# Grouping the last two groups' stores into one transfer of 64 KB pieces, and splitting gamma into two transfers, in an RMSNorm-GELU kernel

## The chip, the cores and the metric

One core of one Trainium2 chip. The metric is the device time of one execution in microseconds (us), as a median over runs; the span in a profile is the same execution seen by the hardware profiler and is about 1.8 us shorter.

## The reference

```python
# x: (8, 1024, 2048) float32, gamma: (2048,), eps = 1e-5
rms = np.sqrt(np.mean(x ** 2, axis=-1, keepdims=True) + eps)
out = gamma * x / rms
return 0.5 * out * (1 + np.tanh(np.sqrt(2 / np.pi) * (out + 0.044715 * out ** 3)))
```

8192 rows of 2048 floats are read once and written once: 67.1 MB in and 67.1 MB out.

## The kernel before

The rows are cut into 16 groups of 512 rows: 128 partitions with 4 rows each, 4 MB. Six slots of 4 MB hold groups in SBUF, as three tiles of two slots. SyncE issues the loads, ScalarE gamma and the stores. Per group, ScalarE and VectorE share the squares, a few small operations give the inverse root, VectorE multiplies by gamma (held in PSUM, spread there by TensorE), ScalarE does the GELU in place, and the slot is stored. The next load into a slot waits for that store.

Two neighbouring groups can be laid out as a pair: each partition then holds 8 consecutive rows, so one transfer of 8 MB moves 64 KB in one piece per partition instead of 32 KB. Before the change that is done for the load of groups 2 and 3 and for the store of groups 12 and 13.

```python
LOAD_PAIR = 1
STORE_PAIR = 6
GW = 128
...
    def part(a, g):
        if g // 2 in (LOAD_PAIR, STORE_PAIR):
            return pair_part(a, g // 2)[:, g % 2 * R : g % 2 * R + R, :]
        return a[g * R * P : (g + 1) * R * P].rearrange("(p r) d -> p r d", p=P)
...
    spare = sbuf.tile([P, D // GW, GW + 16], FP32, name="spare")   # scratch of VectorE's squares
    gamma_row = spare[0:1]                                         # gamma lands there first
...
    def store(g):
        if g:
            if g // 2 != STORE_PAIR:
                nc.scalar.dma_start(out=part(o2, g), in_=slot[g % SLOTS])
            elif g % 2:
                nc.scalar.dma_start(
                    out=pair_part(o2, g // 2), in_=pair[g // 2 % (SLOTS // 2)])
            return
        ...  # group 0: two transfers
...
        for g in range(G + 1):
            if g < G:
                squares(g, 0, R - on_vector(g))
                squares_on_vector(g, R - on_vector(g), on_vector(g))
                ...  # inverse_rms(g), scale(g)
            if g:
                gelu(g - 1)
                store(g - 1)
                if g - 1 + SLOTS < G:
                    load(g - 1 + SLOTS)
```

## Time and profile before

| | before |
|---|---|
| time, median of the first 3 runs | 316.97 us (316.78 to 317.06) |
| span of the profiled run | 315.1 us |
| busiest compute engines | ScalarE 66%, VectorE 63% |
| both DMA queues together | 99.0% of the 16 engines' span |
| bytes moved | 134.24 MB, 426 GB/s over the span |

The row to look at first in such a page is the one of the DMA, because no compute engine comes near its span. In the wait lists, the columns are the engine and line that waited, what it waited for, the sum in us, how often and the longest. Stretches of the DMA ("windows") count a packet wholly where it starts. A packet here is one piece of 32 or 64 KB and takes 1.2 or 2.4 us. Holes were therefore read from the packet records themselves. The lines of the kernel before are in the prediction below.

### The profile page before, as it was taken

How to read it: one execution, taken by the hardware profiler on the slowest of the kernel's cores; microseconds unless marked ns; L12 is line 12 of the kernel's file. 1: busy time of each engine (PE TensorE's matmuls, PEld its weight loads, DVE VectorE, ACT ScalarE, POOL GpSimd, SP SyncE). 2: the span in 40 equal slices, each digit the busy share in tenths (PEclk: the TensorE clock that was granted, in tenths of full speed). 3: DMA queues.
4: the chain of work that ended last, by engine and by line, in shares of the span. 5: the costliest groups of instructions: out<-in, count | busy, mean ns of one | idle time of the engine just before them, and what ended most of it. 6: DMA issues, size and time to landing. Idle time of an engine off the chain costs nothing.

```text
span 315.1 us, 457 instructions
## 1 busy us (share of the span) xinstructions
PE 7.2 (2%) x8; PEld 2.5 (1%) x8; DVE 198.5 (63%) x129; ACT 206.9 (66%) x150; POOL 16.4 (5%) x21
## 2 busy tenths in 40 slices
PE   0900000000000000000000000000000000000000
PEld 0300000000000000000000000000000000000000
DVE  0089887988989884639684393668727638781000
ACT  1327869999999749397590965929369295797000
POOL 0010101011010101010010100101001010010000
DMA  8999989999999999999999999999999999999896
GB/s 334 404 462 408 526 339 396 458 402 462 403 463 403 459 408 458 412 453 424 441 424 441 424 441 424 441 428 437 437 428 437 428 437 428 474 399 474 387 445 291
DMA packets 4498, 134.24 MB, mean 426 GB/s; under 512 B 512, under 2 KB 656, under 8 KB 656
## 3 DMA queue, kind: packets, MB, share of 16 engines
q1 hardware_dynamic: 2160, 67.11, 49.7%
q10 hardware_dynamic: 2336, 67.12, 49.3%
q14 instruction: 2, 0.02, 0.0%
HBM read 67.12 MB, written 67.11 MB: 426 GB/s over the span
## 4 chain that ended last, share of the span: by engine, by line
another core or an unknown queue 36%; DMA 36%; ACT 18%; issue 1%; SPq 1%; ACTq 0%
DMA pair<-in_x_dram 21%; DMA out_dram<-pair 15%; ACT pair L133 12%; ACT junk L87 6%; SPq L83 1%; ACTq L143 0%
## 5 line engine op out<-in xcount | busy, mean ns | idle before, releaser
L124 DVE TENSOR_TENSOR pair<-pair,gamma_ps 128x8192 f32<-128x8192 f32 (+1 forms) x19 | 139.2, 7334 | 0.0
L87 ACT ACTIVATE junk<-pair 128x2048 f32<-128x2048 f32 x42 | 79.0, 1881 | 78.7 <-DMA pair<-in_x_dram 76.2
L133 ACT ACTIVATE pair<-pair,rstd 128x2048 f32<-128x2048 f32 x64 | 122.6, 1987 | 2.3 <-DVE pair L124 1.9
L97 DVE SCALAR_TENSOR_TENSOR spare<-pair 128x2048 f32<-128x2048 f32 x22 | 50.4, 2291 | 39.3 <-DMA pair<-in_x_dram 24.6
L110 POOL TENSOR_TENSOR y<-ms,power 128x4 f32<-128x4 f32 x16 | 16.1, 1007 | 260.8 <-DVE ms L105 260.8
L105 DVE TENSOR_SCALAR ms<-ssq 128x4 f32<-128x4 f32 x16 | 2.7, 170 | 26.2 <-ACT junk L87 25.4
L113 DVE TENSOR_TENSOR z<-ms,y 128x4 f32<-128x4 f32 x16 | 2.6, 163 | 19.0 <-POOL y L110 19.0
L87 ACT ACTIVATION_READ_ACCUMULATOR junk<-pair 128x1 f32 x42 | 7.8, 186 | 0.0
L171 PE MATMUL gamma_ps<-spare,ones 1*128 1x512 f32 x8 | 7.2, 1072 | 8.3 <-DMA spare<-in_gamma_dram 8.3
L117 DVE SCALAR_TENSOR_TENSOR rstd<-z,y 128x4 f32<-128x4 f32 x16 | 2.6, 162 | 0.6
L114 DVE SCALAR_TENSOR_TENSOR z<-z,y 128x4 f32<-128x4 f32 x16 | 2.6, 162 | 0.6
L171 PEld LDWEIGHTS gamma_ps<-spare,ones 1*128 1x128 f32 x8 | 2.5, 326 | 11.4 <-issue 11.4
L169 ACT ACT_TABLE_LOAD x1 | 1.3, 1283 | 1.4 <-PEq L211 1.4
L97 DVE DVE_READ_ACCUMULATOR spare<-pair 128x1 f32 x22 | 1.8, 83 | 0.0
L167 DVE MEMSET warm<- 1x1 f32 x1 | 0.1, 59 | 0.8 <-PEq L211 0.8
L169 ACT ACTIVATE warm<-warm 1x1 f32<-1x1 f32 x1 | 0.2, 202 | 0.0
L168 DVE MEMSET ones<- 1x128 f32 x1 | 0.2, 165 | 0.0
L166 POOL MEMSET power<- 128x4 f32 x1 | 0.1, 101 | 0.3 <-POOLq L211 0.3
L211 POOL MEMSET const-float32-0.0<- 128x1 f32 x1 | 0.1, 98 | 0.2 <-issue 0.2
L211 POOL MEMSET const-bfloat16-1.0<- 128x1 bf16 x1 | 0.1, 102 | 0.0
L211 POOL MEMSET const-uint8-127<- 128x1 uint8 x1 | 0.1, 102 | 0.0
L211 POOL MEMSET const-float32-1.0<- 128x1 f32 x1 | 0.1, 98 | 0.0
## 6 DMA issues: line engine op xcount, KB each, us to landing
pair<-in_x_dram SPq DMA_DIRECT2D x14, 4096.0 KB, 25.5
out_dram<-pair ACTq DMA_DIRECT2D x13, 4096.0 KB, 52.4
out_dram<-pair ACTq DMA_DIRECT2D x1, 4032.0 KB, 31.3
out_dram<-pair ACTq DMA_DIRECT2D x1, 64.0 KB, 17.6
spare<-in_gamma_dram ACTq DMA_DIRECT2D x1, 8.0 KB, 7.4
pair<-in_x_dram SPq DMA_DIRECT2D x1, 40.5
out_dram<-pair ACTq DMA_DIRECT2D x1, 30.9
```

The lines of the kernel that those rows point to most:

```text
L83: nc.sync.dma_start(out=slot[g % SLOTS], in_=part(x2, g))
L87: nc.scalar.activation(out=junk, in_=slot[g % SLOTS][:, q, :], func=ACT.Square, accum_out=ssq[:, g, q : q + 1],)
L97: nc.vector.scalar_tensor_tensor(out=spare[:, :, 0:GW], in0=row, scalar=1.0, in1=row, op0=ALU.bypass, op1=ALU.mult, accum_out=ssq[:, g, q ...
L105: v.tensor_scalar(out=ms, in0=ssq[:, g, :], scalar1=1.0 / D, scalar2=eps_f, op0=ALU.mult, op1=ALU.add,)
L110: nc.gpsimd.tensor_tensor(out=y_, in0=m_, in1=power, op=ALU.pow)
L113: v.tensor_tensor(out=z_, in0=m_, in1=y_, op=ALU.mult)
L114: v.scalar_tensor_tensor(out=z_, in0=z_, scalar=-0.5, in1=y_, op0=ALU.mult, op1=ALU.mult)
L117: v.scalar_tensor_tensor(out=rstd[:, g, :], in0=z_, scalar=1.5, in1=y_, op0=ALU.add, op1=ALU.mult,)
L124: nc.vector.tensor_tensor(out=rows, in0=rows, in1=gamma_ps.unsqueeze(1).to_broadcast([P, n, D]), op=ALU.mult,)
L133: nc.scalar.activation(out=slot[g % SLOTS][:, r, :], in_=slot[g % SLOTS][:, r, :], func=ACT.Gelu_apprx_tanh, scale=rstd[:, g, r : r + 1],)
L169: nc.scalar.activation(out=warm, in_=warm, func=ACT.Gelu_apprx_tanh)
L171: nc.tensor.matmul(out=gamma_ps[:, k : k + 512], lhsT=ones, rhs=gamma_row[:, k // GW : (k + 512) // GW, 0:GW], start=True, stop=True,)
```

## The change

Groups 14 and 15 are stored as a pair, as groups 12 and 13 already are, and gamma is loaded in two halves, with the scratch tile cut to fit. Its intent: fewer and longer pieces at the end, where nothing but stores runs, while the number of transfers stays at 32. The diff is shortened.

```diff
-STORE_PAIR = 6
-GW = 128
+STORE_PAIRS = (6, 7)
+GW = 64
+GAMMA = [(0, 1024), (1024, 2048)]
@@ part
-        if g // 2 in (LOAD_PAIR, STORE_PAIR):
+        if g // 2 in (LOAD_PAIR, *STORE_PAIRS):
@@
-    spare = sbuf.tile([P, D // GW, GW + 16], FP32, name="spare")
+    spare = sbuf.tile([P, D // GW, GW + 8], FP32, name="spare")
@@ store
-            if g // 2 != STORE_PAIR:
+            if g // 2 not in STORE_PAIRS:
@@
-        nc.scalar.dma_start(
-            out=gamma_row[:, :, 0:GW],
-            in_=gamma.rearrange("(o a b) -> o a b", o=1, b=GW),
-        )
+        for a, b in GAMMA:
+            nc.scalar.dma_start(
+                out=gamma_row[:, a // GW : b // GW, 0:GW],
+                in_=gamma[a:b].rearrange("(o a b) -> o a b", o=1, b=GW),
+            )
```

## The prediction

> **What bounds the kernel now.** I read first the shares of the engines, the DMA row over time and the queue table (the page of the kernel before):
>
> ```profile
> PE 7.2 (2%) x8; PEld 2.5 (1%) x8; DVE 198.5 (63%) x129; ACT 206.9 (66%) x150; POOL 16.4 (5%) x21
> DMA  8999989999999999999999999999999999999896
> DMA packets 4498, 134.24 MB, mean 426 GB/s; under 512 B 512, under 2 KB 656, under 8 KB 656
> q1 hardware_dynamic: 2160, 67.11, 49.7%
> q10 hardware_dynamic: 2336, 67.12, 49.3%
> ```
>
> No compute engine is above 66%. The two queues, q1 (loads, issued by SyncE) and q10 (gamma and stores, issued by ScalarE), together fill 49.7 + 49.3 = 99.0% of the 16 DMA engines' span of 315.1 us, so about 3 us of the span (1%) are without transfers. The bytes are fixed: 67.1 MB in, 67.1 MB out.
>
> Second, the waits, of ScalarE and of SyncE's own queue:
>
> ```profile
> ACT junk L87 <- DMA pair<-in_x_dram: 76.2, 12, 10.1
> ACT pair L133 <- DVE pair L124: 1.9, 1, 1.9
> SPq L83 <- DMA out_dram<-pair: 236.9, 11, 47.3
> ```
>
> ScalarE's 78.7 us of idleness before its squares is waiting for loads; the loads wait for stores to free their slots. All of it is the DMA.
>
> Third, the tail, which the change touches: the timeline of ScalarE and its queue, and the DMA share in stretches (columns: stretch, its length, busy time of PE, PEld, DVE, ACT, POOL, clock, DMA share, GB/s).
>
> ```profile
> 264.01 0.34 ACTq L145 DMA_DIRECT2D out_dram<-pair  x1
> ...
> 281.29 0.34 ACTq L143 DMA_DIRECT2D out_dram<-pair  x1
> 281.67 7.68 ACT L133 ACTIVATE pair<-pair,rstd 128x2048 f32<-128x2048 f32 x4 [0.42 <-ACT pair L133]
> 289.38 0.34 ACTq L143 DMA_DIRECT2D out_dram<-pair  x1
> ```
> ```profile
> 264.00:281.00 17.00, 0.00 (x0) 0.00 (x0) 13.01 (x12) 11.32 (x8) 1.01 (x1) 1.00 1.01 436
> 281.00:289.00 8.00, 0.00 (x0) 0.00 (x0) 3.90 (x2) 7.58 (x5) 0.00 (x0) 1.00 1.04 451
> 293.60:313.00 19.40, 0.00 (x0) 0.00 (x0) 0.00 (x0) 0.00 (x0) 0.00 (x0) 1.00 1.00 432
> ```
>
> The store of groups 12 and 13 (8 MB) goes out at 264.0, group 14's at 281.3, group 15's at 289.4, and nothing computes after that. Yet the DMA is full from 264 to 313: the last stores wait behind a backlog. The page's row of issues gives 30.9 us from issue to landing for the 8 MB store, that is 294.9. So the two 4 MB stores, issued at 281.3 and 289.4, cannot begin before about 294.
>
> I then took the packet records (start, length and size of every packet) and chained packets into 16 engines by matching ends to starts. On every engine a packet starts 4 ns before the last one ends; I found no gap above 0.13 us. The engines begin between 1.74 and 2.91 us and end between 312.98 and 313.93 us; they finish the 8 MB store between 293.6 and 294.6 us. The span is thus: 1.74 us to the first byte, some 312 us of packets without a hole, and 1.16 us from the last packet to the end.
>
> [...] a packet of 32,768 bytes takes 1,213 ns, less the 4 ns of overlap, so 27.1 GB/s for one engine and 433.7 for 16. [...] 65,536 bytes take 2,418 ns, two packets of half the size 2,426, so about 8 ns a packet, or 4 ns net of the overlap. [...] gamma's 16 packets of 512 B start at 5.9 to 6.6 us, its 16 completion writes at 7.2 to 7.8, one 32 KB load packet between the two. [...] The page of the kernel before has 2,291 ns for N = 2048 where the output is cut into 16 pieces[...].
>
> **The change part by part.**
>
> *The two last stores become one of 8 MB.* Removed: one issue of 0.34 us on ScalarE at 281.3, and 256 packets of 32 KB. Added: 128 packets of 64 KB. On each engine 16 x (1,213 - 4) = 19,344 ns become 8 x (2,418 - 4) = 19,312 ns: 32 ns less. One completion write per engine goes: 9 - 4 = 5 ns less. Group 14's data now wait for group 15's gelu, some 8 us longer, but this costs only if an engine runs dry first. The last gelu no longer waits for the issue at 281.3: its rows are ready on VectorE at 280.5, 282.7 and 284.9 us, so the four activations of about 1.92 us run from 281.3 to about 289.0. The store is issued at 289.0, done at 289.3. A first packet on an idle queue followed its issue within 1.0 us at the start (0.74 to 1.74), which gives 290.0. The first engine runs out of the 8 MB store at 293.6: 3.6 us to spare. So no hole; -0.04 us at the end.
>
> *The loads of groups 14 and 15* take rows with the stride of the pair: still 128 pieces of 32 KB each, as groups 12 and 13 already have, whose packets took the same 1,213 ns. No cost.
>
> *Gamma in two transfers.* 16 packets of 512 B (27 ns each, one per engine) become 32 of 256 B (about 18 ns, an estimate from 9 ns for a 4-byte packet and 27 for 512 B). Per engine 2 x (18 - 4) - (27 - 4) + 5 for one more completion write = +10 ns. With one load packet between each, as above, the second half's completion comes two load packets after the first's: 2 x 1.2 = 2.4 us, so near 10.2 us, 10.6 as seen by TensorE. The first half feeds the first four of eight matmul records, which at 7.16/8 = 0.9 us keep TensorE busy from 8.3 to 11.8 us. The second half is there by then, and gamma's broadcast still ends at 15.4.
>
> *32 transfers in all.* One store fewer and one gamma transfer more keep the count. The compiled program hands eight completion semaphores out in turn, and a transfer waits for the one eight before it. The comparison of the two programs shows this chain shifted by one place: each late store and load still waits for the same earlier transfer as now. One wait is new: group 5's load waits for gamma's first half (8.2 us instead of an issue at about 2.6). At that moment the loads of groups 0 to 4 still have over 15 MB queued, over 30 us of work.
>
> *The scratch tile in 32 pieces of 64* instead of 16 of 128, same bytes: 22 VectorE squares of 2,291 ns. [...] VectorE is idle for 117 us anyway.
>
> Sum: -0.04 + 0.01 = -0.03 us, a tenth of the spread of three runs (316.78 to 317.06). I predict 316.9 us: no visible change.
>
> **The rivals.**
>
> *The tail gets a hole.* If the store's first packet needed over 4 us from its issue, engines would idle between 293.6 and its arrival. For: the gamma packets of 512 B, issued at 0.74, began only at 5.9, 5.2 us later. [...] At 5.2 us the packets would come at 294.2, a hole of 0.6 us at most: 317.5.
>
> *The held-back store is exposed in full.* On paper 4 MB that could start at 281.3 start at 289.0, a loss of 7.7 us: 324.6. This would need the queue to be empty at 281, and the DMA share of 1.04 for 281 to 289 speaks against it.
>
> *Larger pieces are really faster.* If 64 KB pieces gained 1% over 8 MB, that is 1% of 19.3 us, 0.2 us. The packet records of the 8 MB stores and loads already there give 0.2% per packet. Even then 316.7.
>
> *The beginning shifts.* If TensorE waited for gamma's second half, VectorE would begin up to 2.5 us later, and the first store with it. For: VectorE's first squares did wait 14.4 us for that broadcast. Against: loads fill the DMA until far beyond 40 us and ScalarE then waits for the 8 MB load until 42.1 in any case. Time: unchanged, or +0.3 at most.
>
> **Range and chances.** The span is packets without holes; I can find 0.03 us of them to save and at most 0.6 us to lose. The runs spread by 0.28 us, and the 16 engines' ends differ by 0.95 us. 316.4 to 317.5 should hold it 8 times in 10. Over 2% is 6.3 us: slower by that needs the fully exposed store (1%), faster would need bytes to vanish (1%); within 2%: 98%.
>
> **What would show it.** Packets 4498 - 128 + 16 = 4386, under 512 B 544; a single 8 MB store at about 289.0 landing at about 314; a DMA share of 1.0 from 294 to 313; both queues' shares again summing to 99%; TensorE's last matmul ending near 15.4; the square on VectorE again at 2,291 ns. Wrong would be: a stretch after 293 with the DMA below 0.9 over several us, or a span that moves by more than 1 us.

What the trace before shows: gamma's packets began 5.2 us after their issue behind three load packets on at least 15 of the 16 engines, and the last load packet ends at 268.0 us, 21 us before the last store's issue.

## The result

| | before | after |
|---|---|---|
| time, median of 6 runs | 317.01 us (316.78 to 317.64) | 317.20 us (316.99 to 317.31) |
| span of the profiled run | 315.1 us | 315.2 us |
| packets | 4498 | 4386 |

The ratio is 1.0004, with a 95% interval of 0.9991 to 1.0017: no visible change. Ratios here are the mean time of one kernel's fast runs over that of the other's of the same rounds, so not quite the ratio of the medians quoted.

The page of the changed kernel, its DMA rows:

```profile
DMA  8999989999999999999999999999999999999996
DMA packets 4386, 134.24 MB, mean 426 GB/s; under 512 B 544, under 2 KB 672, under 8 KB 672
q1 hardware_dynamic: 2160, 67.11, 49.7%
q10 hardware_dynamic: 2224, 67.12, 49.3%
```

112 packets are gone, exactly those of the prediction, and nothing else has moved: the same bytes, the same two shares, again 99.0% together. The beginning and the end in the timeline (start, length, engine):

```profile
0.74 1.23 ACTq L165 DMA_DIRECT2D spare<-in_gamma_dram  x2
2.12 6.27 SPq L85 DMA_DIRECT2D pair<-in_x_dram  x2
8.18 7.16 PE L174 MATMUL gamma_ps<-spare,ones 1*128 1x512 f32 x8 [8.18 <-DMA spare<-in_gamma_dram]
15.38 2.29 DVE L99 SCALAR_TENSOR_TENSOR spare<-pair 128x2048 f32<-128x2048 f32 x1 [14.36 <-PE gamma_ps L174]
...
263.94 0.34 ACTq L147 DMA_DIRECT2D out_dram<-pair  x1
273.49 15.23 ACT L135 ACTIVATE pair<-pair,rstd 128x2048 f32<-128x2048 f32 x8
...
288.75 0.34 ACTq L147 DMA_DIRECT2D out_dram<-pair  x1
```

The second line is group 4's load, and group 5's after it, which now has its new wait and is out at 2.12 + 6.27 = 8.39 us: both it and gamma's first half raise the same one of the program's eight completion semaphores (in the trace it is raised from 7.6 to 8.0 us as gamma's first half lands, and next from 74.9 us as group 5 does). The eight last gelus run without a break. Group 14's data now leave at 288.75 instead of 281.29 us, 7.5 us later, and this costs nothing. In the packet records the engines finish the store of groups 12 and 13 between 293.5 and 294.8 us, the last store's packets follow there directly, and the engines end between 312.9 and 314.1 us (before: 313.0 and 313.9). From the last packet to the end of the span it is 1.15 us (before 1.16). The stretches of the tail (columns as in the prediction):

```profile
281.00:289.00 8.00, 0.00 (x0) 0.00 (x0) 3.79 (x2) 7.73 (x5) 0.00 (x0) 1.00 1.10 475
289.00:293.60 4.60, 0.00 (x0) 0.00 (x0) 0.00 (x0) 0.00 (x0) 0.00 (x0) 1.00 0.82 356
293.60:313.00 19.40, 0.00 (x0) 0.00 (x0) 0.00 (x0) 0.00 (x0) 0.00 (x0) 1.00 0.97 422
```

The 0.82 is no hole: it stood there before the change too, and the 64 KB packets that fill this stretch are counted where they start.

SyncE's own waits after the change:

```profile
SPq L85 <- DMA out_dram<-pair: 231.9, 11, 42.4
...
SPq L85 <- DMA spare<-in_gamma_dram: 5.3, 1, 5.3
```

The new wait of 5.3 us is there, and no engine ran dry for it: the loads of groups 0 to 4 were queued.

### The profile page after: what moved, and what is told of

The parts are those of the page before. It is cut to its first block, busy times and chain, and to the rows that moved or that the text cites. A ratio compares the mean times of both kernels' runs of the same rounds, so it can differ in the third digit from the quotient of the medians.

```text
span 315.2 us, 457 instructions
## 1 busy us (share of the span) xinstructions
PE 7.2 (2%) x8; PEld 2.5 (1%) x8; DVE 198.4 (63%) x129; ACT 206.8 (66%) x150; POOL 16.4 (5%) x21
## 2 busy tenths in 40 slices
DMA packets 4386, 134.24 MB, mean 426 GB/s; under 512 B 544, under 2 KB 672, under 8 KB 672
## 4 chain that ended last, share of the span: by engine, by line
DMA 58%; ACT 26%; another core or an unknown queue 6%; issue 2%; SPq 0%; ACTq 0%
DMA pair<-in_x_dram 45%; ACT pair L135 17%; DMA out_dram<-pair 13%; ACT junk L89 9%; SPq L85 0%; ACTq L145 0%
## 5 line engine op out<-in xcount | busy, mean ns | idle before, releaser
L99 DVE SCALAR_TENSOR_TENSOR spare<-pair 128x2048 f32<-128x2048 f32 x22 | 50.4, 2289 | 39.2 <-DMA pair<-in_x_dram 24.6
```

Source lines behind the costliest of these rows:

```text
L99: nc.vector.scalar_tensor_tensor(out=spare[:, :, 0:GW], in0=row, scalar=1.0, in1=row, op0=ALU.bypass, op1=ALU.mult, accum_out=ssq[:, g, q ...
```

## The experiments

The theory: from 1.74 us to the end, all 16 DMA engines carry packets without a hole, so only the time of the packets counts, and an issue may move freely as long as it comes before the queue runs dry. The rivals: the count or order of the transfers matters; the last store is exposed from its issue; longer pieces are really faster; compute sets the pace. Experiments 1 to 8 start from the changed kernel; their diffs are against it, and each time is compared with the kernel before, run in the same rounds.

### 1. The stores alone

```diff
-GW = 64
+GW = 128
-GAMMA = [(0, 1024), (1024, 2048)]
+GAMMA = [(0, 2048)]
@@
-    spare = sbuf.tile([P, D // GW, GW + 8], FP32, name="spare")
+    spare = sbuf.tile([P, D // GW, GW + 16], FP32, name="spare")
```

> Only the second 8 MB store, gamma in one transfer, so 31 transfers in all. Theory (the DMA engines carry packets without a hole from first byte to last, so only packet time counts): 0.04 us less than the kernel before, not visible: ratio 1.000 within 0.001; the packet records show 128 packets of 64 KB more on the store queue. Rival (the count of 32 transfers matters, because it shifts which earlier transfer each one waits for): a hole in the DMA and a time at least 1 us above.

Measured: 317.27 us against 316.97 us for the kernel before in the same rounds, ratio 1.001 (0.9997 to 1.0023). The packet records show no hole. The rival's 1 us did not come; with 31 transfers the kernel runs as with 32.

### 2. Gamma alone

```diff
-STORE_PAIRS = (6, 7)
+STORE_PAIRS = (6,)
```

> Only gamma in two transfers and the scratch tile in pieces of 64; stores as in the kernel before; 33 transfers. Theory: ratio 1.000 within 0.001; gamma's second half lands near 10.2 us, TensorE still ends at 15.3 to 15.5, group 5's load is issued near 8.4 us without a hole. Rival (the 0.2 us by which the changed kernel's median lies higher comes from the beginning): this kernel shows it, a ratio of 1.0005 or more, and the stores alone do not.

Measured: 317.13 us against 316.97 us, ratio 1.0006 (0.9993 to 1.0018), with 33 transfers. TensorE ended at 15.50 us and group 5's load was issued by 8.54 us, with no hole in the packet records. The ratio passes the rival's 1.0005, but the stores alone came out no lower, so the rival's second condition fails. Each half lies 0.1 to 0.3 us above the kernel before at the median and each interval holds 1. Whether the change costs a tenth of a microsecond or nothing is below what these rounds resolve, and stays open.

### 3. How late may the last store leave?

Squares whose result nobody reads are put between the last gelu and the last store, two or four of them, later seven (the number in the loop):

```diff
                 gelu(g - 1)
+                if g == G:
+                    for _ in range(2):
+                        nc.scalar.activation(out=junk, in_=slot[0][:, 0, :], func=ACT.Square)
                 store(g - 1)
```

> The changed kernel with two more ScalarE squares (2.0 us each) between the last gelu and the last store, which is thus issued near 292.8 instead of 288.75. The first engine runs out of the store before it at 293.5. Theory with a latency of 1.0 us from issue to first packet (as at the start of the kernel): packets at 293.8, a hole of 0.2 to 0.3 us, time at most 317.5. Rival (latency near 5 us, as gamma's packets had): packets at 298, a hole of over 4 us, time 321 or more. If the last store were exposed from its issue on: +4.0 us.

> The same with four squares: the last store issued near 296.8, some 3.3 us after the first engine has run out. Theory: the hole is 296.8 + 1.0 - 293.5 = 4.3 us on the first engine and, as the last engine ends the store before it at 294.8, about 3.0 us on that one; all engines restart together, so the end moves to about 297.8 + 8 x 2.41 = 317.1 + 1.2, span 318.3, time about 320.2, +3.0 us. Rival (latency 5 us): +7 us. Rival (exposed from the issue on): +8 us.

Measured: 317.07 us with two (ratio 1.0004, 0.9989 to 1.0019) and 317.91 us with four (1.0029, 1.0015 to 1.0043), against 316.97 us. The second is +0.9 us where I had expected +3.0. The timelines with two and with four squares:

```profile
288.62 3.77 ACT L197 ACTIVATE junk<-pair 128x2048 f32<-128x2048 f32 x2
290.51 0.34 ACTq L147 DMA_DIRECT2D out_dram<-pair  x1
```
```profile
288.67 7.60 ACT L197 ACTIVATE junk<-pair 128x2048 f32<-128x2048 f32 x4
294.40 0.34 ACTq L147 DMA_DIRECT2D out_dram<-pair  x1
```

My count was wrong, not the model: the store goes out when the last square begins, not when it ends (1.9 us earlier, in all three runs with squares); it uses no result of the squares. With four squares it left at 294.40 instead of 296.8. The packet records have 4 or more of the 16 engines idle from 293.64 to 295.34 us. The first packet came at 295.24 us, 0.84 us after the issue, the last engine's at 295.39. From there 8 packets of 2.414 us and the 1.16 us at the end give 295.34 + 19.3 + 1.16 = 315.8; the span was 316.0. With two squares the store left at 290.51, too early for any hole, so only four and seven squares test the limit.

As that was reckoned after the fact, a run with seven squares was foretold from it:

> The changed kernel with seven squares before the last store. With two and four squares the store was issued at 290.51 and 294.40, one square earlier than I had counted: the issue waits only for the last gelu's completion and leaves while the last square still runs. So seven squares put it at 288.75 + 6 x 1.94 = 300.3. Theory (the store's first packet follows its issue by 0.95 us, as with four squares, and 8 packets of 2.414 us follow without a hole): last packet at 300.3 + 0.95 + 19.3 = 320.5, span 321.7, time 323.5, +6.5 us, a hole from 293.6 to 301.2. Rival (some other floor of the last store): not this sum.

Measured: 323.52 us against 317.00 us, ratio 1.0202 (1.0187 to 1.0218), span 321.7 us: the foretold numbers. Timeline and stretches (start and end, length, busy time of PE, PEld, DVE, ACT, POOL, clock, DMA share, GB/s):

```profile
288.63 13.33 ACT L197 ACTIVATE junk<-pair 128x2048 f32<-128x2048 f32 x7
300.09 0.34 ACTq L147 DMA_DIRECT2D out_dram<-pair  x1
```
```profile
293.60:300.90 7.30, 0.00 (x0) 0.00 (x0) 0.00 (x0) 7.17 (x5) 0.00 (x0) 1.00 0.00 0
300.90:320.50 19.60, 0.00 (x0) 0.00 (x0) 0.00 (x0) 1.06 (x1) 0.00 (x0) 1.00 0.99 428
```

A DMA share of 0.00 for 7.3 us is what an exposed store looks like. The first packet again came 0.84 us after the issue. So a hole begins to open where the issue comes later than about 293.55 - 0.84 = 292.7 us (an estimate). The change issues at 288.75 us and leaves about 4 us unused. The time itself follows the slowest engine, which leaves the store before at 294.8 us and not at 293.6. It should therefore begin to lengthen only about 1 us later still. That fits the four squares: some engines were idle for up to 1.8 us, but the last packet ended at 314.80 instead of 314.10 us.

### 4. The store of groups 12 and 13 held back too

```diff
-                store(g - 1)
+                if g - 1 != 13:
+                    store(g - 1)
+                if g == G:
+                    store(13)
```

> The changed kernel with the store of groups 12 and 13 also held back to after the last gelu: both 8 MB stores are issued near 288.8 and 289.1. What the change does to 4 MB is here done to 12 MB and should meet an empty queue. In the changed kernel the first store's packets run from about 274.5 on, so the queue should be dry from 274.5 until 289.8. Theory: a hole of about 15 us, then 16 x 2.41 = 38.6 us, end of packets near 328.5, time about 331.5, ratio 1.046. Rival (the chip is bound by bytes over the whole span, whatever the order): no change.

Measured: 331.45 us against 317.01 us, ratio 1.0459 (1.0441 to 1.0476). The timeline's store issues and the stretches:

```profile
288.47 0.82 ACTq L147 DMA_DIRECT2D out_dram<-pair  x2
```
```profile
274.60:289.20 14.60, 0.00 (x0) 0.00 (x0) 8.60 (x8) 13.84 (x8) 1.01 (x1) 1.00 0.00 0
289.20:328.20 39.00, 0.00 (x0) 0.00 (x0) 0.00 (x0) 0.00 (x0) 0.00 (x0) 1.00 1.00 430
```

The hole lies where it was expected (274.4 to 289.4 us in the packet records) and its 15 us are lost almost whole: +14.4 us. It is the same edit in kind as the change. Only the backlog in the queue made the one free and the other dear.

### 5. The cost of a packet, enlarged

The 4 ns that the change saves per pair of packets cannot be seen, so the other direction was tried: the last 8 MB in many small pieces, as two transfers of even and odd pieces (d = 512 floats for 2 KB, 128 for 512 B).

```diff
+            elif g == G - 1:
+                for h in range(2):
+                    nc.scalar.dma_start(
+                        out=pair_part(o2, 7).rearrange(
+                            "p r (c h d) -> p h (r c) d", h=2, d=512)[:, h],
+                        in_=pair[1].rearrange(
+                            "p r (c h d) -> p h (r c) d", h=2, d=512)[:, h],
+                    )
             elif g % 2:
```

> The last 8 MB leave in pieces of 2 KB (two transfers, even and odd pieces; 33 transfers in all) instead of 64 KB. From the packet records (256 B 18 ns, 512 B 27, 32 KB 1213, 64 KB 2418) a packet costs 8 to 9 ns and 27.2 GB/s, less an overlap of 4 ns. Theory: 256 packets of about 79.5 ns per engine, 20.3 us instead of 19.3: +1.0 us, time about 318.2. Rival (only bytes count): no change. [...]

Measured: 318.50 us against 317.01 us, ratio 1.0044 (1.0029 to 1.0059), the span 1.3 us above that of the changed kernel. The packet records have 84 ns for each piece of 2 KB, against 83.5 expected, and one every 80 ns on each engine. That is 256 x 80 = 20.5 us against 19.3, or about 410 GB/s for 16 engines, with no gap above 0.03 us. A second rival: issuing so many pieces sets the pace. No engine ran dry here; the two issues took ScalarE's queue 9.19 us.

> The same in pieces of 512 B. Theory: 1024 packets of 27 - 4 = 23 ns per engine, 23.6 us instead of 19.3: +4.2 us, time about 321.4, ratio 1.013. [...]

Measured: 324.93 us, ratio 1.0250 (1.0234 to 1.0265), +7.9 us where +4.2 was expected. The stretches of the tail:

```profile
293.50:301.50 8.00, 0.00 (x0) 0.00 (x0) 0.00 (x0) 0.00 (x0) 0.00 (x0) 1.00 1.08 327
301.50:306.00 4.50, 0.00 (x0) 0.00 (x0) 0.00 (x0) 0.00 (x0) 0.00 (x0) 1.00 1.05 303
306.00:320.00 14.00, 0.00 (x0) 0.00 (x0) 0.00 (x0) 0.00 (x0) 0.00 (x0) 1.00 1.02 291
```

From 295 to 301.5 us, when every engine is past the store before, a packet starts every 23.6 ns on each engine, near the expected 23, and later every 28.2 ns, about 347 and 291 GB/s for 16 engines; the engines are busy throughout. (Packets overlap, by 4 ns in the kernel before, so the share passes 1; the first stretch has fewer GB/s because the last 64 KB packets are still under way in it.) +7.9 us is as good as the number on record of the rival cut, that issuing sets the pace. The two issues took ScalarE's queue 16.33 us, until 305.1, but the slow pace began near 302 us and outlives them until 321, which speaks against this rival without excluding it. Why the pace fell was not found out. The cost per packet is thus shown to be real and of the size supposed at 2 KB (84 ns against 83.5); at 512 B the time per packet was larger, for a reason that stays open. Between 32 and 64 KB it is 4 ns of 2.4 us, too small to be seen.

### 6. Half of the last store

Wrong on purpose: group 15 is never written.

```diff
+            elif g == G - 1:
+                nc.scalar.dma_start(
+                    out=pair_part(o2, 7)[:, 0:R, :], in_=pair[1][:, 0:R, :]
+                )
             elif g % 2:
```

> Wrong on purpose: of the last 8 MB only the first half of each partition's rows (group 14) is stored, in pieces of 32 KB, at the same moment. Theory (the DMA is full up to the end, so each byte taken off the tail ends the kernel earlier): 4 MB less is 8 x 1.209 = 9.67 us less, time about 307.5, ratio 0.9695. Rival (something else than bytes sets the end, such as a fixed latency of the last store): a smaller gain.

Measured: 307.48 us against 317.01 us, ratio 0.9703 (0.9686 to 0.9719), the expected time. The 4 MB taken off the tail were worth 9.5 us, against 9.67 us of packet time. The change takes off none.

### 7. VectorE with half its work

Wrong on purpose: the multiplication by gamma is left out for groups 1 to 11.

```diff
-                    scale(g, 0, R)
+                    if not 1 <= g <= 11:
+                        scale(g, 0, R)
```

> Wrong on purpose: the multiplication by gamma is left out for groups 1 to 11, which takes 11 x 8.68 = 95 us of work from VectorE (198 us busy). Theory (no compute engine is on the path in the middle of the kernel): time 317.0 within 0.5 us, the DMA without holes as before. Rival (compute decides when the slots come free and the kernel gains from it): faster by several us.

Measured: 317.16 us against 317.02 us, ratio 1.0008 (0.9992 to 1.0025). The page's row of engines and the group of the multiplication:

```profile
PE 7.2 (2%) x8; PEld 2.5 (1%) x8; DVE 104.1 (33%) x118; ACT 206.8 (66%) x150; POOL 16.4 (5%) x21
L126 DVE TENSOR_TENSOR pair<-pair,gamma_ps 128x8192 f32<-128x8192 f32 (+1 forms) x8 | 43.7, 5480 | 0.0
```

VectorE fell from 198.4 to 104.1 us busy and the time stayed. VectorE does not set the pace there. ScalarE, 66% busy, was not cut; that it does not either rests on the packet records without a hole.

### 8. Pairs wherever possible

```diff
-LOAD_PAIR = 1
-STORE_PAIRS = (6, 7)
+LOAD_PAIRS = (1, 2, 3, 4, 5, 6)
+STORE_PAIRS = (1, 2, 3, 4, 5, 6, 7)
@@ load (and the first six loads likewise)
+        if g // 2 not in LOAD_PAIRS:
             nc.sync.dma_start(out=slot[g % SLOTS], in_=part(x2, g))
+        elif g % 2:
+            nc.sync.dma_start(
+                out=pair[g // 2 % (SLOTS // 2)], in_=pair_part(x2, g // 2))
@@ part: LOAD_PAIR becomes *LOAD_PAIRS
```

> Pairs wherever they are possible: loads of groups 2 to 13 and stores of groups 2 to 15 in 64 KB pieces. Theory on packets alone: 80 pairs of 32 KB packets per engine become 64 KB packets, 80 x 4 = 320 ns less, time 316.8, ratio 0.999. Rival: stores leave later and slots come free in pairs only, so an engine queue runs dry, most likely between 75 and 95 us where the first loads have ended and the second pair's store is not yet issued: a hole of several us there, time 320 or more. I hold the hole for likelier than the gain.

Measured: 340.28 us against 317.02 us, ratio 1.0737, but the result was wrong: group 14's load went into group 8's slot before the paired store of groups 8 and 9 had been issued. The mended kernel issues the loads of groups 14 and 15 after that store:

```diff
-                if g - 1 + SLOTS < G:
+                if g - 1 + SLOTS < G - 2:
                     load(g - 1 + SLOTS)
+                elif g - 1 + SLOTS == G - 1:
+                    load(G - 2)
+                    load(G - 1)
```

> The all-pairs kernel with its error mended: the first all-pairs kernel loaded group 14 over group 8's result before the paired store had read it. Here the loads of groups 14 and 15 follow the store of groups 8 and 9. Theory: correct, and as slow as the one with the error or slower, 338 to 345 us, with holes in the DMA where loads have ended and the next paired store is not yet issued; packets shorter by 0.3 us in all cannot make up for them.

Measured: correct, 341.21 us (338.87 to 342.35) against 317.00 us, ratio 1.0745 (1.0694 to 1.0796). The page's DMA row and some stretches:

```profile
DMA  8998989998999969999798989899889989489895
```
```profile
122.90:125.90 3.00, 0.00 (x0) 0.00 (x0) 1.42 (x1) 1.36 (x1) 0.00 (x0) 1.00 0.78 262
293.00:298.50 5.50, 0.00 (x0) 0.00 (x0) 5.50 (x1) 5.09 (x4) 0.00 (x0) 1.00 0.00 0
```

Where the row of the changed kernel is nearly all nines, this one is dented in many places. The packet records have seven stretches, from 80.8 to 318.8 us, with 4 or more engines idle, 18.6 us in all. Besides, the packets themselves took 320.3 us per engine instead of 312.2: pieces of 64 KB took 2,509 ns on average instead of 2,418. The average hides that the usual packet is no slower: the median is still 2,418 ns, and 156 of the 159 packets above 2,540 ns (of 1,664, the longest 4,632 ns) lie in eight bursts of 14 to 32 packets, five of them within 3 us of the end of a hole. The holes were expected, the slower packets not, and their cause was not looked for. The 0.3 us to be had from longer packets is far smaller than either.

No experiment points to a version that beats both kernels.

## Why the prediction was right

*What bounds the kernel.* Right, and shown from two sides: 4 MB less in the tail was worth 9.5 us (experiment 6), 94 us less work on VectorE nothing (experiment 7). The prediction put all of ScalarE's 78.7 us of idleness down to loads; its own line has 76.2 of them.

*The two stores as one.* Right. The packets of 64 KB again took 2,418 ns, and no hole opened. The reckoned spare room was 3.6 us with an issue at 289.0. The issue came at 288.75, and experiment 3 puts the limit near 292.7. The latency of 1.0 us taken from the beginning was 0.84 us in the tail (experiments 3 and 4, first packet).

*Gamma in two transfers.* Right: the packets of 256 B took 18 ns; the second half's completions were written at 9.7 to 10.2 us (expected near 10.2); TensorE ended at 15.34 us (expected 15.4).

*Group 5's load.* Right: issued by 8.39 us, without a hole.

*The scratch tile in pieces of 64.* Right: VectorE's squares took 2,289 ns, before 2,291. That 32 pieces cost no more than 16 is what the two traces show.

*The count of transfers.* The prediction gave it no effect; 31 and 33 transfers ran within 0.1% of 32.

*The rivals.* The beginning did not shift: VectorE's first square began at 15.38 us, before at 15.46. The hole in the tail did not open in the change, but it was made at will: 7.3 us of it with seven squares. The exposed store failed for the reason given, a full queue at 281 us (DMA share 1.10 from 281 to 289); with an empty one it cost 14.4 us of a hole of 15 (experiment 4). Longer pieces were faster by 4 ns for each two pieces of 32 KB joined, and no more.

*The sum.* -0.03 us was predicted, +0.2 us measured at the median, with an interval from -0.3 to +0.5 us: neither tells the sign. In the packet records the saving drowns too: an engine's packets sum to 312.21 us before and 312.23 after, as the 32 KB loads took 0.7 ns more on average. That the time stayed was foretold for the right reason; that 0.03 us was saved is not shown. One sign of the list read a little off: the DMA share of the stretch from 293.6 to 313 us is 0.97 instead of 1.0, because a window counts a packet where it starts and the packets have doubled in length. The packet records have no hole there.

## What to carry to other kernels

Where the DMA row is full from end to end, ask of a change first whether it takes bytes or packets away and what one packet costs; here joining two pieces of 32 KB saved 4 ns of 2.4 us. Then ask how long the queue would last without the transfer that the change delays: a delay shorter than the backlog, less the 0.84 us from issue to first packet, is free here, and of a longer one the excess was paid nearly in full (14.4 of 15 us in experiment 4). When there is nothing to see in the changed direction, enlarge the suspected cost until it is seen.
